# A 1 KB transfer from x into the output on ScalarE's queue ahead of the opening barrier, in a DMA-bound add + LayerNorm kernel

## Chip, cores, metric

One core of one Trainium2 chip. The metric is device time of the core in microseconds (us). Before: 238.15 us, the median of three runs (238.14 to 238.19). The span of a profile is about 1.2 us shorter than the device time of the same run (236.9 against 238.26), because it starts at the first recorded instruction. SyncE is called SP in the profile, GpSimd POOL, VectorE DVE and ScalarE ACT. HBM is the memory outside the core, which holds x, residual and the output; on-chip memory is the core's SBUF, which holds `zbuf` and `rbuf`. The opening barrier is the point at which all engines wait for each other before the kernel's own instructions start.

## The reference

```python
# x, residual: (16, 1024, 512) float32; gamma, beta: (512,); eps = 1e-5
z = x + residual
mean = np.mean(z, axis=-1, keepdims=True)
var = np.var(z, axis=-1, keepdims=True)
return (gamma * (z - mean) / np.sqrt(var + eps) + beta).astype(np.float32)
```

64 MiB are read (x and residual) and 32 MiB written.

## The kernel before

All large transfers stand in one list, in the order in which SyncE issues them. `x16+16` loads row blocks 16 to 31 of x (a row block is 128 rows, 256 KB), `r` is residual, `o` is a store. 16 row blocks are 4 MB: 32 KB on each of 128 partitions, hence eight packets of 32 KB on each of the 16 DMA engines.

```python
PLAN = """
x0+8 r0+8 x8+8 r8+8 x16+16 r16+16 x32+16 r32+16
x48+16 r48+16 o0+16 r64+16 x64+16 o16+16 r80+16 x80+16
o32+16 r96+16 x96+8 x104+8 o48+16 r112+16 x112+8 x120+8
o64+16 o80+16 o96+16 o112+12 o124+4
"""
EARLY = 2        # so many of SyncE's issues are moved ahead of the opening barrier
# ...
for k, src in enumerate((gamma, beta)):
    nc.scalar.dma_start(out=gb_row[:, k * D : (k + 1) * D], in_=src[None, :]).then_inc(s_gb[k], 16)
# ...
def move(out, in_, s):
    i = nc.sync.dma_start(out=out, in_=in_).then_inc(s, 16)
    if len(first) < EARLY:
        first.append(i.ins)

for kind, lo, n in moves:
    if kind == "x":      # ... waits until the store that frees these rows of zbuf has landed
        move(part(zbuf, Z_ROWS, lo, n), dram(xf, lo, n), sx[...])
    elif kind == "r":
        wait_rows(s_add, "add", lo + n - R_ROWS)     # GpSimd has added the rows that stood here
        move(part(rbuf, R_ROWS, lo, n), dram(rf, lo, n), sr[...])
    else:
        wait_rows(s_out, "out", lo + n)              # VectorE has finished these rows
        move(dram(of, lo, n), part(zbuf, Z_ROWS, lo, n), so[...])
# ... GpSimd: zbuf += rbuf; ScalarE: mean, sum of squares, sqrt; VectorE: the rest, in zbuf
# ... at the end: the instructions in `first` are moved ahead of the opening barrier
```

## Time and profile before

| | before |
|---|---|
| median of the first three runs | 238.15 us |
| share of 16 DMA engines' span, SyncE's queue | 99.2% |
| rate over the span | 425 GB/s |
| ScalarE, VectorE, GpSimd busy | 78%, 75%, 60% |

The first lines are from the page of the kernel before: DMA busy in tenths over 40 slices and its rate in each, then the DMA queues (packets, MB, share).

```profile
DMA  8999999999999999999999999999999999999996
GB/s 310 443 432 426 426 443 443 443 443 443 426 415 398 443 443 443 426 420 409 431 437 443 443 443 432 420 407 429 443 437 437 409 432 448 437 420 437 426 430 285
...
DMA packets 4181, 100.68 MB, mean 425 GB/s; under 512 B 466, under 2 KB 466, under 8 KB 468
...
q1 hardware_dynamic: 4176, 100.67, 99.2%
...
q10 hardware_dynamic: 4, 0.00, 0.0%
```

The queue of SyncE (q1) never rests. So the kernel is bound by the DMA engines, and what can be won is only the time in which they run below their rate. ScalarE's queue (q10) carries gamma and beta alone.

The opening, from the timeline of the kernel before (start us, us, engine, line, operation):

```profile
0.00 0.38 SPq L146 DMA_DIRECT2D zbuf<-in_x_dram  x1
...
0.43 0.42 SPq L146 DMA_DIRECT2D rbuf<-in_residual_dram  x1
1.91 0.33 SPq L146 DMA_DIRECT2D zbuf<-in_x_dram  x1
1.92 0.52 ACTq L124 DMA_DIRECT2D gb_row<-in_gamma_dram  x1
```

The third and fourth lines are the first work behind the barrier. x0's first packet begins at 1.0 us, 0.62 us after its issue ended. The Trainium skill (DMA: Bandwidth & Descriptors, "Latency and other measured facts") has the first byte of such a transfer at about 0.6 us; this agrees.

Windows of the kernel before (window, its length, busy time and count of PE, PEld, DVE, ACT, POOL, clock, DMA share, GB/s):

```profile
70.00:76.00 6.00, 0.00 (x0) 0.00 (x0) 5.73 (x11) 5.68 (x18) 6.00 (x1) 1.00 1.00 431
76.00:80.00 4.00, 0.00 (x0) 0.00 (x0) 3.40 (x7) 3.89 (x13) 2.81 (x1) 1.00 0.95 369
80.00:86.00 6.00, 0.00 (x0) 0.00 (x0) 5.70 (x12) 5.70 (x17) 5.33 (x2) 1.00 0.99 426
```

369 GB/s stands where the first store, o0, follows r48 in the queue. Such a window must be read with care: packets of 32 KB end in waves of 16 about every 1.2 us, and one wave more or less changes a window of 4 us by a third. The packet records of the trace are safer. They say that the packets around it take 1.21 us, and r48's last two or three on each engine, at 77.0 to 79.7 us, up to 1.68 us.

From here on **excess** means: packet duration minus 607 ns per 16 KB, summed over the packets of a stretch and divided by 16 engines. "Ahead of o0" sums the packets that start in the last 3.9 us before the transfer in front of o0 ends on the first engine to finish it. "At the start" sums those that start within 1.5 us of x0's first. These sums come from the packet records of the kept traces; no view printed here lists the packets. In the kernel before the excess ahead of o0 is 0.38 us. At the start it is 0.70 us: x0's first packets take 1.10 to 1.47 us instead of 0.61.

### The profile page before, as it was taken

How to read it: one execution, taken by the hardware profiler on the slowest of the kernel's cores; microseconds unless marked ns; L12 is line 12 of the kernel's file. 1: busy time of each engine (PE TensorE's matmuls, PEld its weight loads, DVE VectorE, ACT ScalarE, POOL GpSimd, SP SyncE). 2: the span in 40 equal slices, each digit the busy share in tenths (PEclk: the TensorE clock that was granted, in tenths of full speed). 3: DMA queues.
4: the chain of work that ended last, by engine and by line, in shares of the span. 5: the costliest groups of instructions: out<-in, count | busy, mean ns of one | idle time of the engine just before them, and what ended most of it. 6: DMA issues, size and time to landing. Idle time of an engine off the chain costs nothing.

```text
span 236.9 us, 1471 instructions
## 1 busy us (share of the span) xinstructions
PE 3.7 (2%) x4; PEld 1.2 (0%) x4; DVE 177.2 (75%) x290; ACT 185.5 (78%) x545; POOL 143.0 (60%) x29
## 2 busy tenths in 40 slices
PE   0600000000000000000000000000000000000000
PEld 0100000000000000000000000000000000000000
DVE  0001977939699999999898989896989895698920
ACT  2019879497999999999999998979998956999300
POOL 0098920999799699604995059944995049950000
DMA  8999999999999999999999999999999999999996
GB/s 310 443 432 426 426 443 443 443 443 443 426 415 398 443 443 443 426 420 409 431 437 443 443 443 432 420 407 429 443 437 437 409 432 448 437 420 437 426 430 285
DMA packets 4181, 100.68 MB, mean 425 GB/s; under 512 B 466, under 2 KB 466, under 8 KB 468
## 3 DMA queue, kind: packets, MB, share of 16 engines
q1 hardware_dynamic: 4176, 100.67, 99.2%
q14 instruction: 1, 0.01, 0.0%
q10 hardware_dynamic: 4, 0.00, 0.0%
HBM read 67.11 MB, written 33.55 MB: 425 GB/s over the span
## 4 chain that ended last, share of the span: by engine, by line
DMA 71%; POOL 9%; ACT 9%; DVE 2%; issue 2%; SPq 1%; ACTq 0%; DVEq 0%; POOLq 0%
DMA out_dram<-zbuf 49%; DMA rbuf<-in_residual_dram 16%; POOL zbuf L180 9%; DMA zbuf<-in_x_dram 6%; ACT junk_s L212 5%; ACT junk_m L202 4%; SPq L146 1%; DVE zbuf L240 1%; DVE zbuf L252 1%; ACTq L202 0%; DVEq L240 0%; ACT std L221 0%; DVE rstd L249 0%; ACTq L193 0%; POOLq L177 0%
## 5 line engine op out<-in xcount | busy, mean ns | idle before, releaser
L180 POOL TENSOR_TENSOR zbuf<-zbuf,rbuf 128x2048 f32<-128x2048 f32 (+1 forms) x25 | 142.8, 5740 | 67.6 <-DMA zbuf<-in_x_dram 40.8
L240 DVE SCALAR_TENSOR_TENSOR zbuf<-zbuf,nm,gamma_p 128x512 f32 x128 | 87.1, 743 | 46.3 <-ACT junk_s L212 46.3
L202 ACT ACTIVATE junk_m<-zbuf 128x512 f32 x128 | 74.9, 585 | 29.1 <-POOL zbuf L180 27.5
L212 ACT ACTIVATE junk_s<-zbuf,nm 128x512 f32 x128 | 88.8, 694 | 1.0
L252 DVE SCALAR_TENSOR_TENSOR zbuf<-zbuf,rstd,beta_p 128x512 f32 x128 | 87.1, 743 | 1.1
L212 ACT ACTIVATION_READ_ACCUMULATOR junk_s<-zbuf,nm 128x1 f32 x128 | 23.9, 187 | 0.0
L202 ACT ACTIVATION_READ_ACCUMULATOR junk_m<-zbuf 128x1 f32 x128 | 23.9, 187 | 0.0
L221 ACT ACTIVATE std<-ssq,eps_t 128x4 f32<-128x4 f32 x32 | 9.5, 297 | 3.0
L249 DVE RECIPROCAL rstd<-std 128x4 f32<-128x4 f32 x32 | 5.5, 170 | 0.0
L190 ACT ACT_TABLE_LOAD x1 | 1.3, 1283 | 2.7 <-PEq L60 2.7
L132 PE MATMUL gamma_p<-gb_row,ones 1*128 1x512 f32 x2 | 2.0, 1119 | 7.2 <-DMA gb_row<-in_gamma_dram 7.2
L132 PE MATMUL beta_p<-gb_row,ones 1*128 1x512 f32 x2 | 1.9, 1052 | 0.0
L127 DVE MEMSET ones<- 1x128 f32 x1 | 0.2, 165 | 2.0 <-PEq L60 2.0
L132 PEld LDWEIGHTS beta_p<-gb_row,ones 1*128 1x128 f32 x2 | 0.7, 328 | 1.0 <-issue 0.5
L132 PEld LDWEIGHTS gamma_p<-gb_row,ones 1*128 1x128 f32 x2 | 0.5, 308 | 7.1 <-issue 7.1
L288 POOL MEMSET const-float32-0.0<- 128x1 f32 x1 | 0.1, 98 | 0.2 <-issue 0.2
L288 POOL MEMSET const-bfloat16-1.0<- 128x1 bf16 x1 | 0.1, 101 | 0.0
L288 POOL MEMSET const-uint8-127<- 128x1 uint8 x1 | 0.1, 101 | 0.0
L288 POOL MEMSET const-float32-1.0<- 128x1 f32 x1 | 0.1, 98 | 0.0
L128 DVE MEMSET eps_t<- 128x1 f32 x1 | 0.1, 59 | 0.0
## 6 DMA issues: line engine op xcount, KB each, us to landing
rbuf<-in_residual_dram SPq DMA_DIRECT2D x7, 4096.0 KB, 30.5
out_dram<-zbuf SPq DMA_DIRECT2D x7, 4096.0 KB, 28.6
zbuf<-in_x_dram SPq DMA_DIRECT2D x5, 4096.0 KB, 28.9
zbuf<-in_x_dram SPq DMA_DIRECT2D x6, 2048.0 KB, 14.9
rbuf<-in_residual_dram SPq DMA_DIRECT2D x2, 2048.0 KB, 15.7
out_dram<-zbuf SPq DMA_DIRECT2D x1, 3072.0 KB, 13.5
out_dram<-zbuf SPq DMA_DIRECT2D x1, 1024.0 KB, 10.2
gb_row<-in_gamma_dram ACTq DMA_DIRECT2D x1, 2.0 KB
```

Source lines behind the costliest of these rows:

```text
L127: nc.vector.memset(ones[:, :], 1.0).then_inc(s_const, 1)
L132: nc.tensor.matmul(dest[:, :], ones[:, :], gb_row[:, k * D : (k + 1) * D], start=True, stop=True).then_inc(s_pe, 1)
L146: i = nc.sync.dma_start(out=out, in_=in_).then_inc(s, 16)
L180: nc.gpsimd.tensor_tensor(out=z, in0=z, in1=part(rbuf, R_ROWS, lo, n), op=ALU.add).then_inc(s_add, n)
L190: act.preload_act_table_set("sqrt_and_others")
L202: i = act.activation(out=junk_m[k][:, :], in_=zk[k], func=ACT.Identity, scale=-inv_d, accum_out=nm[j][:, k : k + 1],)
L212: i = act.activation(out=junk_s[k][:, :], in_=zk[k], func=ACT.Square, bias=nm[j][:, k : k + 1], accum_out=ssq[j][:, k : k + 1],)
L221: act.activation(out=std[j][:, :], in_=ssq[j][:, :], func=ACT.Sqrt, bias=eps_t[:, 0:1], scale=inv_d,).then_inc(s_std, TURN)
L240: dve.scalar_tensor_tensor(out=zk[k], in0=zk[k], scalar=nm[j][:, k : k + 1], in1=gamma_p[:, :], op0=ALU.add, op1=ALU.mult,)
L249: dve.reciprocal(out=rstd[j][:, :], in_=std[j][:, :]).then_inc(s_dve, TURN)
L252: i = dve.scalar_tensor_tensor(out=zk[k], in0=zk[k], scalar=rstd[j][:, k : k + 1], in1=beta_p[:, :], op0=ALU.mult, op1=ALU.add,)
L288: nc = _bacc.Bacc("TRN2", target_bir_lowering=False, num_devices=1)
```

## The change

The intent: whatever the first write to the output costs is to be paid early, by a 16 x 16 piece of x (16 rows of 64 B) copied into rows that o0 later writes over. This copy is called the touch. Two writes to the same bytes must not race, so o0 waits for it.

```diff
+TOUCH = 16
...
+    s_touch = sem("touch")
...
+    touch = nc.scalar.dma_start(out=of[0:TOUCH, 0:TOUCH], in_=xf[0:TOUCH, 0:TOUCH])
+    touch.then_inc(s_touch, 16)
     for k, src in enumerate((gamma, beta)):
...
-        if len(first) < EARLY:
+        if len(first) <= EARLY:
             first.append(i.ins)
+    first.append(touch.ins)
...
         else:
+            if lo == 0:
+                nc.sync.wait_ge(s_touch, 16)
             wait_rows(s_out, "out", lo + n)
```

## The prediction

> **What bounds the kernel.** The DMA engines. The page gives queue 1 99.2% of 16 engines' span, 425 GB/s over 100.68 MB. ScalarE (78%), VectorE (75%) and GpSimd (60%) wait for data (the wait table: GpSimd 40.8 us on x, 26.8 us on residual). The last 1 MB store is issued at 226.7 us and lands 10.2 us later, behind a 3 MB store: a backlog, not compute. So the time is bytes over the full rate, plus every moment in which the engines run below it.
>
> **Where they run below it** (the trace's packet records, duration minus the usual 607 ns per 16 KB, averaged over the engines):
> - The start: first packet 1.0 us after the issue at 0.00; the first packets take 1.15 to 1.47 us instead of 0.61. Excess 0.68 us.
> - Just before the first store: another transfer of 4 MB takes 9.7 us on an engine, but the last two or three packets of r48, directly ahead of o0 in the queue, take up to 1.68 us instead of 1.21 (77.0 to 79.7 us); it takes 9.9 to 10.15. Excess 0.38 us. The table of windows has 369 GB/s for 76:80, against 421 to 431 around it. No later change from loads to stores shows it, so I read it as the cost of the first write to the output in an execution (inferred from its timing, not shown).
>
> **What the change does.** One 16x16 transfer (16 rows of 64 B) goes out before the barrier. By the Trainium skill (DMA: Bandwidth & Descriptors, "Why a DMA increments its semaphore by 16 and not by 1"), the engine count is the largest divisor up to 16 of the slowest dims, so all 16 engines get one row each and meet the output early. The trace agrees only for the large transfers (16 semaphore packets each). The instruction order shows nothing else moved: one issue on ScalarE before its barrier, one wait on SyncE.
>
> **Cost.**
> - Bytes: 1 KB; a 2 KB gamma packet takes 84 ns, so under 0.1 us per engine. The same page ("Issuing engines are not separate DMA queues") says ScalarE's transfers share the same 16 engines; so the touch can delay x0's first packets. If its write cost is paid in series there, the gain is cancelled; I expect most of it to overlap the cold first reads.
> - Issue on ScalarE: 0.52 us (gamma's, first on that queue). SyncE's two early issues last until 0.85 us, so the barrier should hardly move, and loads behind it queue after x0 and r0 (landed at 11.8 us). Gamma and beta may come up to 0.5 us later; GpSimd's first sum isn't done before 17 us. Off the path.
> - The first store's wait: satisfied long before 59.8. One more wait, under 0.1 us, with transfers queued. Free.
>
> **On the critical path:** 0.38 us saved at 77 us, carried to the end because the queue never empties; less 0.05 to 0.3 us at the start. Net about -0.3 us, 0.13%.
>
> **Prediction:** 237.85 us, range 237.4 to 238.3. Faster by over 2%: 0.01; within 2%: 0.98; slower by over 2%: 0.01.
>
> **What would show it:** r48's last packets back at 1.21 us and 76:80 at about 425 GB/s; the first x packets as before or slightly longer; o0 and every later landing about 0.3 us earlier; barrier end within 0.1 us of 1.9.
>
> **What would make it wrong:** the slow packets at 77 us are not the first write's (no gain); each part of the output has its own first cost (no gain); the touch stalls the engines longer than the cold reads do (x0 lands later, even or slower); ScalarE's issue holds the barrier up; or the touch, arriving before x0, pays part of the cold reads too (down to 237.3).

## The result

238.19 us, the median of six runs (238.05 to 238.65), against 238.14 (238.08 to 238.32) for six runs of the kernel before. The ratio is 1.0005, with a 95% interval of 0.9992 to 1.0018: the same. The interval, about 0.2 us down and 0.4 us up, excludes the forecast gain of 0.3 us (a ratio of 0.9987).

The page of the changed kernel, the same parts:

```profile
DMA  8999999999999999999999999999999999999996
GB/s 310 435 421 429 443 443 443 443 443 437 415 404 426 443 443 421 415 426 432 432 443 443 443 432 426 426 409 432 443 443 437 407 421 445 432 443 421 443 422 293
...
DMA packets 4213, 100.68 MB, mean 425 GB/s; under 512 B 498, under 2 KB 498, under 8 KB 500
...
q1 hardware_dynamic: 4176, 100.67, 99.2%
q10 hardware_dynamic: 36, 0.01, 0.0%
...
out_dram<-in_x_dram ACTq DMA_DIRECT2D x1, 1.0 KB, 6.6
```

ScalarE's queue has 32 packets more: 16 of 64 B and 16 for the semaphore. So the touch did go to all 16 engines, as the Trainium skill (DMA: Bandwidth & Descriptors, "Why a DMA increments its semaphore by 16 and not by 1") has it for a slowest dimension of 16. The last line says that it took 6.6 us from issue to landing.

The opening, from the timeline of the changed kernel:

```profile
0.00 0.38 SPq L152 DMA_DIRECT2D zbuf<-in_x_dram  x1
0.12 0.63 ACTq L127 DMA_DIRECT2D out_dram<-in_x_dram  x1
...
0.43 0.42 SPq L152 DMA_DIRECT2D rbuf<-in_residual_dram  x1
2.09 0.33 SPq L152 DMA_DIRECT2D zbuf<-in_x_dram  x1
2.10 0.49 ACTq L130 DMA_DIRECT2D gb_row<-in_gamma_dram  x1
```

ScalarE's issue ends at 0.75 us, and the work behind the barrier starts 0.18 us later than before. It costs nothing, since those loads stand behind x0 and r0 in the queue. The touch's packets of 64 B come at 4.84 to 5.24 us and the last of them at 5.72, not at the start: x0's first packets run at 1.0 us in both kernels, with an excess of 0.69 against 0.70 us.

The windows of the changed kernel:

```profile
70.00:76.00 6.00, 0.00 (x0) 0.00 (x0) 5.74 (x10) 5.68 (x18) 6.00 (x2) 1.00 0.96 415
76.00:80.00 4.00, 0.00 (x0) 0.00 (x0) 3.41 (x6) 3.91 (x13) 2.92 (x1) 1.00 0.98 385
80.00:86.00 6.00, 0.00 (x0) 0.00 (x0) 5.72 (x11) 5.68 (x18) 5.23 (x2) 1.00 1.01 437
```

The dip is still there (385 GB/s). By packets, the excess ahead of o0 is 0.37 us against 0.38 us, although every engine had written to the output 72 us earlier. What was to be saved was not saved. So the question is what these slow packets are.

### The profile page after: what moved, and what is told of

Read it like the earlier page. It is cut to its first block, busy times and chain, and to the rows that moved or that the text cites. A ratio compares the mean times of both kernels' runs of the same rounds, so it can differ in the third digit from the quotient of the medians.

```text
span 236.9 us, 1473 instructions
## 1 busy us (share of the span) xinstructions
PE 3.7 (2%) x4; PEld 1.2 (0%) x4; DVE 177.2 (75%) x290; ACT 185.5 (78%) x545; POOL 143.0 (60%) x29
## 3 DMA queue, kind: packets, MB, share of 16 engines
q1 hardware_dynamic: 4176, 100.67, 99.2%
## 4 chain that ended last, share of the span: by engine, by line
DMA 71%; POOL 9%; ACT 9%; DVE 2%; issue 2%; SPq 1%; ACTq 0%; DVEq 0%; POOLq 0%
DMA out_dram<-zbuf 49%; DMA rbuf<-in_residual_dram 16%; POOL zbuf L189 9%; DMA zbuf<-in_x_dram 6%; ACT junk_s L221 5%; ACT junk_m L211 4%; SPq L152 1%; DVE zbuf L249 1%; DVE zbuf L261 1%; ACTq L211 0%; DVEq L249 0%; ACT std L230 0%; DVE rstd L258 0%; ACTq L202 0%; POOLq L186 0%
```

## The experiments

Twelve runs, each made once with a profile (state unknown; times only to a few tenths of a us, for the kernel before took 238.19 to 238.69 in its single runs beside them). One of them, `b1_before`, is the kernel before itself. They all gave correct results. The e and b runs ran on one chip and the f runs on another. All the others but `f2_touch_alone` are edits of the kernel before. Extra transfers "between r8 and x16" are put into SyncE's list ahead of x16, and SyncE waits for them ahead of a later transfer: o0 in e2 to e4, r32 in b2 and f3 to f5. Letters such as "theory A" or "rival B" are those of the expectations.

### Does the slow spot follow the first store? e1_swap

```diff
-x48+16 r48+16 o0+16 r64+16 x64+16 o16+16 r80+16 x80+16
+x48+16 r48+16 r64+16 o0+16 x64+16 o16+16 r80+16 x80+16
```

> Issue order changed: r64 goes ahead of the first store o0, so o0 follows r64 instead of r48 in SyncE's queue. Theory A (the slow packets belong to the first large store, paid just ahead of it): r48 takes its usual 9.7 us per engine, and the last two or three packets of r64 (about 87 us) are the slow ones, excess about 0.38 us averaged over the engines. Rival B (the place belongs to r48, to its addresses or to the moment 77 us): r48's last packets stay slow at 77 to 79.7 us and r64's end is normal. The total may be longer by some us, since r64 now waits for GpSimd and x64 for o0 closer to the end of the queue.

243.6 us. Windows of this run:

```profile
71.00:77.00 6.00, 0.00 (x0) 0.00 (x0) 5.53 (x9) 5.71 (x17) 6.00 (x1) 1.00 0.98 421
77.00:80.00 3.00, 0.00 (x0) 0.00 (x0) 2.72 (x5) 2.88 (x10) 1.82 (x1) 1.00 1.18 448
...
88.00:92.00 4.00, 0.00 (x0) 0.00 (x0) 3.40 (x6) 3.88 (x14) 4.00 (x2) 1.00 0.94 295
92.00:98.00 6.00, 0.00 (x0) 0.00 (x0) 5.70 (x11) 5.71 (x17) 6.00 (x1) 1.00 1.01 437
```

The spot followed the store: r48 ended normally (excess 0.01 us), r64's last packets were slow. But the excess had grown to 1.12 us. It came a second time too, 1.03 us ahead of o16, where the kernel before has none (x64 takes 9.68 us there). The two places have one thing in common. The queue had just run dry, or nearly so, and the load between the restart and the store was the first one. (r64 was issued when r48 had almost ended: from 79.44 to 80.54 us fewer than 16 packets were in flight, but never none. x64 was issued only after o0 had landed: no packet was in flight from 101.7 to 103.0 us.) Rival B falls, and so does "once per execution".

### Do small touches on the exact rows of o0 pay it? e2_sb_out, e3_x_out, e4_sb_sb

```diff
+        if (kind, lo) == ("x", 16):        # e2: on-chip -> output, 64 KB (scr is set to 0 by VectorE, SyncE waits for that)
+            nc.sync.dma_start(out=dram(of, 0, 1)[:, 0:128], in_=scr[:, 0:128]).then_inc(s_touch, 16)
# e3: x -> output
+            nc.sync.dma_start(out=dram(of, 0, 1)[:, 0:128], in_=dram(xf, 0, 1)[:, 0:128]).then_inc(s_touch, 16)
# e4: on-chip -> on-chip
+            nc.sync.dma_start(out=scr[:, 128:256], in_=scr[:, 0:128]).then_inc(s_touch, 16)
```

> Kernel before plus a small store from on-chip memory (128 rows of 512 B, to the first row of every partition's part of o0) on SyncE's own queue, between r8 and x16 (about 21 us), o0 waits for it. Theory A1 (a first store from on-chip memory pays once per execution, the touch of the change failed because it read HBM, used another queue or touched only 16 rows): slow packets move to about 19 to 21 us (excess 0.3 to 0.4 us there), the end of r48 at 77 to 79.7 is normal (under 0.1 us). Rival B: 77 to 79.7 unchanged at 0.37 us. Total time about equal to before in both cases (within 0.5 us).

> As the run before, same place, queue and rows of the output, but its source is x in HBM (128 rows of 512 B). If the cost is of writing to these places of the output, the slow packets move to about 21 us and 77 to 79.7 is normal; if it is of reading on-chip memory by the DMA engines for the first time, 77 to 79.7 keeps its 0.37 us. Rival B: keeps it too.

> As the two before, but from on-chip memory to on-chip memory, the output isn't touched. If the cost is of the first read of on-chip memory, it moves to about 21 us and 77 to 79.7 is normal; if it is of the first write to the output, 77 to 79.7 keeps its 0.37 us. Rival B: keeps it too.

238.48, 238.47 and 238.38 us. None of them made packets slow at about 21 us. Ahead of o0 the excess was 0.34, 0.35 and 0.12 us. So touching each partition's part of o0, on SyncE's own queue and from either kind of memory, doesn't pay it: theory A1 falls. The 0.12 of e4 looked like an effect of reading on-chip memory. To see what chance does, the kernel before was profiled again.

### The spread of the spot itself: b1_before

No edit.

> The kernel before once more, for the spread of the slow spot itself: two profiles (before, after) gave 0.37 and 0.38 us for the last packets of r48, the four runs since gave 0.12 to 0.36. If this one gives 0.3 to 0.4, the 0.12 us of the run with the on-chip transfer may mean something; if it gives another value under 0.25, it is chance.

238.57 us, excess ahead of o0 0.85 us. The window of this run:

```profile
77.00:81.00 4.00, 0.00 (x0) 0.00 (x0) 3.66 (x7) 3.88 (x14) 1.83 (x1) 1.00 1.06 377
```

(Of the "four runs" of the expectation three are on record with such a value, e2 to e4; e1 had 1.12.) Neither branch of the expectation foresaw a value this high. In profiles without any bulk disturbance of the stream, then, the spot costs 0.12 to 0.85 us, and one profile can't tell 0.12 from 0.38. By the same measure the 0.37 of the changed kernel would not by itself show that the touch saved nothing; that rests on the times, and that no write to the output is needed rests on f3 below.

### A full-size store early: b2_big_store

```diff
+        if (kind, lo) == ("x", 16):
+            nc.sync.wait_ge(sr[0], 16)
+            nc.sync.dma_start(out=dram(of, 0, 8), in_=part(rbuf, R_ROWS, 0, 8)).then_inc(s_touch, 16)
```

> A full-size store of 2 MB is put between r8 and x16, at about 21 us. Theory C (the cost belongs to the first change from streaming loads to streaming stores after the queue has started from idle; a transfer of a few KB doesn't count as one): r8's last packets are slow (excess 0.3 us or more at 19 to 22 us), r48's at 77 to 85 are normal (below 0.1 us). Rival F (it belongs to r48 and o0, by addresses or place): nothing at 21 us, 0.3 to 0.4 us ahead of o0. Rival G (phases of the 16 engines against each other): either. Total: 4.9 us longer for the extra bytes.

243.74 us. Windows of this run:

```profile
13.00:19.00 6.00, 0.00 (x0) 0.00 (x0) 0.00 (x0) 1.92 (x7) 6.00 (x2) 1.00 1.01 434
19.00:22.00 3.00, 0.00 (x0) 0.00 (x0) 0.00 (x0) 2.97 (x10) 2.31 (x1) 1.00 0.99 279
22.00:26.00 4.00, 0.00 (x0) 0.00 (x0) 3.17 (x6) 3.87 (x12) 2.85 (x1) 1.00 0.98 418
```

r8's last packets now lose 1.05 us, and ahead of o0 the excess is 0.01 us. The cost can be moved, then, by a bulk store. Rival F (r48 and o0 themselves) falls. Prepaying cost more than leaving it alone: the run is 5.4 us longer than the kernel before beside it, and 4.9 of these are the 2 MB (eight packets of 611 ns on each engine).

### A disturbance without a store: b3_dephase

```diff
+        if (kind, lo) == ("x", 32):
+            for p, at_, s in ((8, 48, s_touch), (4, 56, s_touch2)):
+                nc.sync.dma_start(out=zbuf[0:p, at_ * D : (at_ + 8) * D],
+                    in_=xf[0 : 8 * p, :].rearrange("(p j) d -> p (j d)", p=p)).then_inc(s, 16)
```

> No store added, no idle: two loads on 8 and on 4 partitions (16 KB each) ahead of x32 push half of the engines back by 0.6 us and a quarter by 1.2 us, 39 us ahead of o0. Rival G (the engines run in step after the start and hit the same places at the first store): the excess ahead of o0 changes clearly (under 0.15 us, or over 0.6). Theory C: it stays at 0.3 to 0.4 us. Total: up to 1.2 us longer.

242.0 us. Windows of this run:

```profile
40.00:46.00 6.00, 0.00 (x0) 0.00 (x0) 5.74 (x10) 2.90 (x9) 3.51 (x1) 1.00 0.97 186
46.00:60.00 14.00, 0.00 (x0) 0.00 (x0) 9.08 (x15) 11.52 (x34) 14.00 (x3) 1.00 1.01 435
74.00:80.00 6.00, 0.00 (x0) 0.00 (x0) 5.36 (x10) 5.88 (x18) 6.00 (x2) 1.00 1.01 437
80.00:85.00 5.00, 0.00 (x0) 0.00 (x0) 4.74 (x9) 4.68 (x15) 3.57 (x1) 1.00 0.99 426
```

The two loads, 192 KB in all, cost far more than their bytes: the excess between 40.5 and 46 us was 3.2 us, with packets of up to 4.3 us in the two loads and in x32 behind them. I had expected 1.2 us at most, and the experiment is rougher than it was meant to be. But afterwards the excess ahead of o0 was 0.01 us, without any store before o0. So theory C in its strict form (only a first bulk store ends it) falls as well. The run doesn't tell whether the shifted phases or the large stall ended it.

### Does it come back with a restart? b4_gap

```diff
+        if (kind, lo) == ("x", 48):
+            nc.sync.wait_ge(sr[loads_r.index((32, 16))], 16)
```

> SyncE waits until r32 has landed before it issues x48, so the queue runs dry at about 60 us and starts again, two transfers (x48, r48) ahead of o0. Theory C with an amount that falls with the loads in between: the excess ahead of o0 lies between 0.38 us (ten transfers after the start) and 1.1 us (one transfer, in the run with r64 ahead of o0). If it only depends on being first: 0.3 to 0.4 us. Rival F: 0.3 to 0.4 us. Besides, a restart cost like the start's, 0.7 us or more, at 61 to 63 us. Total: 2 to 3 us longer.

241.53 us. Windows of this run:

```profile
60.00:64.00 4.00, 0.00 (x0) 0.00 (x0) 3.37 (x6) 3.97 (x13) 3.00 (x1) 1.00 0.71 229
78.00:84.00 6.00, 0.00 (x0) 0.00 (x0) 5.74 (x11) 5.68 (x18) 0.96 (x2) 1.00 0.99 350
```

The queue ran dry at 60.4 us and started again at 61.8, its first packets taking up to 2.28 us instead of 1.21. The excess ahead of o0, two loads later, was 1.07 us, as high as with one load in between. Together with e1, where the cost came back at o16 although on-chip memory had been read before, this says that the state in which the cost is due comes from starting out of idle. The fall with the number of loads that I had guessed isn't clean: two loads cost as much as one, and the runs with ten loads spread from 0.12 to 0.85 us.

### The touch with the engines to itself: f2_touch_alone

```diff
-EARLY = 2
+EARLY = 0     # edit of the changed kernel
```

> The changed kernel with EARLY = 0: x0 and r0 are issued after the barrier, so the touch has the 16 DMA engines to itself. If the touch ran late in the changed kernel (4.8 us) because it stood behind x0's packets, its packets now start about 1 us after its issue, ahead of x0's. If x0's slow first packets (1.15 to 1.47 us for 16 KB, excess 0.70 us) are a first contact with x that a touch can pay, x0's excess falls under 0.3 us; if they are the filling of an empty pipeline, it stays at 0.6 to 0.8 us. The slow packets ahead of o0 stay in any case (0.1 to 0.9 us). Total: about 2 us longer than before, since x0 starts after the barrier.

240.11 us against 238.19 beside it. From the timeline and the DMA table of this run:

```profile
0.13 0.63 ACTq L127 DMA_DIRECT2D out_dram<-in_x_dram  x1
...
2.07 0.38 SPq L152 DMA_DIRECT2D zbuf<-in_x_dram  x1
```

```profile
out_dram<-in_x_dram ACTq DMA_DIRECT2D x1, 1.0 KB, 1.9
```

Issued at the same moment, the touch landed after 1.9 us instead of 6.6, and its packets ran at 1.52 to 1.70 us, ahead of x0's. So in the changed kernel it had stood behind x0. x0's first packets still had an excess of 0.56 us. That is neither under 0.3 nor within 0.6 to 0.8. The thirteen other profiles, in none of which a touch ran ahead of x0, have 0.56 (b3) to 0.72 us (e4), so 0.56 is at the edge of their spread: no part of the slow start is shown to be a first contact with x that a touch could pay. Ahead of o0 the excess was 0.34 us, as ever.

### Reading on-chip memory, or writing HBM? f3_big_sb_sb, f4_big_x_out, f5_mid_store

```diff
# each behind the same wait for sr[0] as in b2
# f3: 2 MB on-chip -> on-chip
+            nc.sync.dma_start(out=part(zbuf, Z_ROWS, 48, 8), in_=part(rbuf, R_ROWS, 0, 8)).then_inc(s_touch, 16)
# f4: 2 MB x -> output
+            nc.sync.dma_start(out=dram(of, 0, 8), in_=dram(xf, 0, 8)).then_inc(s_touch, 16)
# f5: 256 KB on-chip -> output
+            nc.sync.dma_start(out=dram(of, 0, 1), in_=part(rbuf, R_ROWS, 0, 1)).then_inc(s_touch, 16)
```

> A 2 MB copy from on-chip memory to on-chip memory between r8 and x16, no write to the output. The run with a 2 MB store there paid 1.0 us at 19 to 22 us and nothing ahead of o0. Theory S (the cost belongs to the change from reading HBM to reading on-chip memory): the same here, about 1.0 us at 19 to 22 us, under 0.1 us ahead of o0. Theory W (it belongs to writing HBM in bulk): nothing at 19 to 22 us, 0.1 to 0.9 us ahead of o0. Theory D (any big disturbance of the stream re-orders the engines for good, as the loads on few engines did): pays something at 20 us and nothing ahead of o0.

> A 2 MB copy from x to the output in HBM between r8 and x16, no read of on-chip memory. Theory S: no slow packets ahead of it, 0.1 to 0.9 us ahead of o0. Theory W: about 1.0 us around 19 to 22 us, under 0.1 us ahead of o0.

> A store of 256 KB (128 rows of 2 KB) between r8 and x16. The 64 KB store there neither paid nor prepaid, the 2 MB store paid 1.0 us and prepaid all. If the size decides: something between, that is part of the cost at 19 to 22 us and the rest ahead of o0; if any store of full-rate packets does it, about 1.0 us at 19 to 22 us and nothing ahead of o0.

243.66, 245.13 and 239.0 us. The same window of the three runs, f3, f4, f5 in this order, each in its own fence:

```profile
19.00:22.00 3.00, 0.00 (x0) 0.00 (x0) 0.00 (x0) 2.97 (x9) 2.19 (x1) 1.00 0.99 268
```

```profile
19.00:22.00 3.00, 0.00 (x0) 0.00 (x0) 0.00 (x0) 2.97 (x10) 2.37 (x1) 1.00 0.97 415
```

```profile
19.00:22.00 3.00, 0.00 (x0) 0.00 (x0) 0.00 (x0) 2.97 (x10) 2.38 (x1) 1.00 0.92 365
```

f3 writes nothing to the output and yet pays as the large store did (1.13 us), with 0.01 us left ahead of o0. f4 writes 2 MB to the output, and the packets ahead of it are normal (0.03 us). It has a cost of its own instead: the copy itself runs slowly in its second half (excess 0.77 us in the last 3.9 us before its end on the last engine), and the first packets of x16 behind it take up to 3.45 us; from 21 to 29 us the excess is 1.29 us in all. Ahead of o0 it leaves 0.17 us, which lies inside the spread of 0.12 to 0.85 and so tells nothing. Theory W (bulk writes to HBM) falls: it wanted about 1.0 us around the copy, which a slow copy might pass for, but f3 has the cost with no such write. Theory S (the change from reading HBM to reading on-chip memory) is what b2, f3 and f4 agree on. Theory D of the expectation (any big disturbance orders the engines anew for good) is not excluded: it foresaw the same outcome of f3, b3 fits it and not S, and f4, a big disturbance too, left a value that tells nothing. What S alone explains is the place of the slow packets, ahead of an on-chip read (b2, f3) and not ahead of the copy from HBM (f4). f5 lies between: 0.18 us at 21 us and 0.26 us ahead of o0, and it alone has 0.16 us more ahead of o16, without a restart. 256 KB is not enough.

All in one table. "Ahead of the extra" is the load in front of the extra transfer:

| run | queue's loads since it started from idle | excess ahead of the extra | excess ahead of o0 |
|---|---|---|---|
| before; b1 | 10 | none | 0.38; 0.85 |
| after (touch at 4.8 us); f2 (at 1.5 us) | 10 | none | 0.37; 0.34 |
| e2, e3, e4: 64 KB extra | 10 | under 0.03 | 0.34, 0.35, 0.12 |
| f5: 256 KB store | 10 | 0.18 | 0.26 |
| b2: 2 MB store | 10 | 1.05 | 0.01 |
| f3: 2 MB on-chip copy | 10 | 1.13 | 0.01 |
| f4: 2 MB copy x to output | 10 | 0.03 | 0.17 |
| b3: loads on few engines | 10 | 3.2 in the loads and x32 | 0.01 |
| b4: queue dry before x48 | 2 | none | 1.07 |
| e1: queue dry before r64 | 1 | none | 1.12 (o16: 1.03) |

## Why the prediction came out as it did

The time lay in the range and in the class that I gave 0.98. That is no merit of the argument: the range, up to 238.3 us, takes in the unchanged 238.15 as well, and no effect at all lands in it. The gain of 0.3 us didn't come, and the step that failed is the one that the gain rested on.

- **"I read it as the cost of the first write to the output in an execution"**: wrong. The term was 0.38 us saved; it measured 0.01 (0.38 to 0.37), far inside the spread of the spot. The runs put in its place: the slow packets stand ahead of the first bulk transfer that reads on-chip memory after the queue has started from idle. They don't need a write to the output (f3), come again after the queue has run dry (e1) and aren't paid by small transfers (the touch, e2, e3). My evidence had been that no later store shows it. That was true, but "first" had several meanings: first write, first store, first read of on-chip memory, first disturbance since the start. I picked one.
- **"all 16 engines get one row each and meet the output early"**: right in number (32 more packets), but early meant 4.84 us and later, behind x0's first packets. In f2 it was 1.5 us, and the excess ahead of o0 (0.34 us) stayed in the spread.
- **"less 0.05 to 0.3 us at the start"**: not seen in x0's first packets (excess 0.69 against 0.70 us). r0, the second load, had landed on the last engine 0.13 us later (11.94 against 11.82 us), but the other profiles with the same start have 11.74 to 11.90 us, so a cost of this size isn't told from none. Since the touch came behind the cold packets there was nothing for it to overlap. The last packet ends at 236.37 us in the changed kernel and at 236.41 in the one before.
- **Barrier, wait, and what bounds**: the barrier moved by 0.18 us instead of at most 0.1, off the path as predicted. SyncE's issue of o0 moved from 59.78 to 59.94 us, with the end of r32 still running and x48 and r48 queued ahead. The DMA share stayed at 99.2%.

That a later gain is carried to the end was never tested by an edit, because there was no gain. Chance gives a hint: b1 had 0.47 us more ahead of o0 than the kernel before, and its last packet ended 0.31 us later (236.72 against 236.41 us). b2 fits it from the other side: 4.9 us of bytes plus 1.05, less the 0.38 to 0.85 not paid later, is 5.1 to 5.6 us (estimate from the numbers above), and it was 5.4 us longer.

What stays open is the mechanism. By the Trainium skill (DMA: Bandwidth & Descriptors, "Two DMAs through the same engine are not ordered") an engine's read and write sides are separate queues. It fits that the packets in front of o0 slow down, and not o0's own: the read side may already be at o0 while r48 is still being written. That is argued and not shown. Nor is it shown why the cost is due only once after a start, why b3 ended it without any read of on-chip memory (the strongest reason to keep theory D), and why the same kernel pays 0.38 in one profile and 0.85 in another. No version beats the two kernels: each transfer that removes the spot costs more than the spot.

## What to carry to other kernels

When a slow spot occurs once, list everything that is "first" at that moment, and move each of them alone before building a remedy for one. Then look for the cost where the warm-up was put: in these runs the small transfers had no slow packets around them (0.03 us or less in e2 to e4), and they prepaid nothing that could be seen. In these runs (e1, b4) a DMA queue that ran dry paid twice, 0.65 to 0.74 us when it started again and 1.03 to 1.12 us at the next bulk read of on-chip memory, so a gap cost more than its idle time.

## What the Trainium skill lacked or had wrong

- DMA: Bandwidth & Descriptors, "Queues, rings and completion order", says that an engine takes turns between its queues packet by packet. Once the touch on ScalarE's queue was being served, this agrees: fifteen of its 64 B packets ran at 4.84 to 5.24 us, the last at 5.72, and the semaphore packets about 0.6 us later (5.45 to 5.85 and 6.33), the time of one packet of SyncE's queue (0.61 us). What the page lacks is the wait for the first turn: issued by 0.75 us, the touch was served only after some five packets of 16 KB of SyncE's queue on each engine (80 packets had started before 4.84 us), while alone it ran at 1.52 us (f2). Why is open; this isn't shown to be an error of the page, whose packet of several descriptors may not be the profile's.
- No page has the cost of starting a queue from idle: an excess of 0.56 to 0.72 us at the start of the kernel (14 profiles), with first packets of 16 KB at up to 1.6 us instead of 0.61, and 0.65 to 0.74 us at a restart (e1, b4).
- No page has the loss ahead of the first bulk read of on-chip memory after such a start: 0.12 to 0.85 us after ten loads, 1.03 to 1.13 us after one or two large loads or four small ones. Ahead of later stores without a restart it is 0.08 us or less, but for 0.16 us in f5.
- DMA: Bandwidth & Descriptors warns in its "Rules for kernel authors" that a small outermost dimension confines a transfer to few engines, but not of the size of the effect on a busy queue: loads on 8 and on 4 partitions, 192 KB in all, brought 12 semaphore packets instead of 32, as the page has it, and an excess of 3.2 us on the mean of the engines (b3).
